# A fused two-block network on one Trainium2 core: the second score product on 128 rows, the shared buffer of the gating unit, and norm weights queued behind linear attention

## The chip, the core and the metric

One core of a Trainium2 chip runs the whole program in one launch. The metric is the device time of that launch in microseconds, the median over several runs. The core's engines are TensorE (PE in the profile, PEld for its weight loads), VectorE (DVE), ScalarE (ACT), GpSimd (POOL) and SyncE (SP), which here issues the DMAs. Each engine works through its own queue in order; the order is fixed when the program is built.

## What is computed

Two blocks follow each other on 256 tokens of width 1024.

- **First block**, two layers, on 256 latent tokens (x) and 256 context tokens (ctx). Each layer projects the modulated input and has three branches: softmax attention (8 query heads, 2 key/value heads of width 64), gated linear attention in both directions ("gla", 4 heads), and a spatial gating unit ("sgu"). The branches are multiplied with gates and summed ("merge"), projected, added to the residual and layer-normalised. In layer 0 latent and context rows are all kept (512 rows); layer 1 keeps the 256 latent rows only.
- **Second block**: forgetting attention, a linear recurrence, and a mixture of 32 experts whose weights (three matrices of 1 MB each) are all read from memory.

What the change touches, in the reference's words:

```python
def attend(q, k, v):
    s = jnp.einsum('btgrd,blgd->bgrtl', q, k, preferred_element_type=jnp.float32) * (ATTN_HEAD_DIM ** -0.5)
    p = jax.nn.softmax(s, axis=-1)
    return jnp.einsum('bgrtl,blgd->btgrd', p.astype(v.dtype), v)

y_sgu = sgu(s_u, s_v, ...) * jax.nn.silu(s_g)     # sgu: pu * (w_s @ layer_norm(pv) + b_s)
x_new = layer_norm(DEEPNORM_ALPHA * x + gate[:, None, :] * out, p['post_g'], p['post_b'])
```

## The kernel before

A large product keeps float32 accuracy by splitting each operand into a high part in the type fp32r and a low part (what is left), and adding three products: high x high, high x low, low x high. The weights are split on the core: ACT writes the high part (`whi`, L97), DVE or POOL subtracts (`wlo`, L98).

**Scores.** `attn_kv` (L531) makes the transposed keys. `kh` has the high part of both key heads; head h lies on 64 of the 128 rows, and POOL copies it to the other 64 (L547). `kl`, the low part, lies on its own 64 rows alone. `attn_core` (L626) takes 128 queries at a time (`tt`: four times in layer 0, twice in layer 1) and puts their high part on one half of the rows of `qs` and the low part on the other. Then there are four rounds (`r`) for each tt. A round makes the scores of two heads (g = 0, 1): one product with `kh` on 128 rows, which is high x high plus low x high at once (L644), and one with `kl` on 64 rows (L646). Softmax follows (DVE L651, L652, ACT L654, DVE L655, L656), four transposes per head (`trp`, PE L659), their copy (`pt`, ACT L661), and eight products with the values (`aops`, PE L666; each shows as two instructions). There are two buffers each for scores, softmax rows, transposes and copies. In layer 0, tt 0 and 1 look at 512 keys and tt 2 and 3 at 256; in layer 1 both look at 512. In all there are 24 rounds and 48 pairs of score products, 32 pairs with 512 columns and 16 with 256.

**Linear attention.** `gla_pair` takes two heads at a time and goes through eight levels (`LEVELS` and the diagonal): POOL (L827, L828, L830), ACT and DVE make the operands, PE the products `attps` (L841), DVE merges them (`accd`, L852). Then come the outputs `gops` (L863, L867) and per head a norm: ACT `osq` (L873), DVE `oms` (L875), POOL `ors` (a power, L222), DVE `on` (L879), POOL `on` (times the gate, L880), and PE transposes (`tro`, L883).

**Gating unit.** `sgu_core` makes `mxps` on PE (L950) for each tt, and both of the two `gm` banks of PSUM are taken by the products of two tt. DVE takes them into `mx` (L954, four instructions per tt), POOL multiplies (L957), ACT and DVE split the result into `ysg` (L958, L959).

**Merge.** `merge` runs twelve steps in the order of the string "s0 s1 s2 g0 g1 g2 a0 s3 g3 a1 a2 a3". A step has 48 gate products `mgps`, in two `gm` banks, and 24 branch products `brps`, on lines L247 to L249; s reads `ysg`, g reads `ygl`, a reads the attention's result.

**Norm weights.** While layer 1's merge begins, `first_block` (L1176, L1177) multiplies the residual x2 with the weights of layer 0's norm and adds its offset: four POOL instructions on 128x1024.

**What sets the order.** The program is written as a sequence, but the framework reorders it when it builds: each engine's queue is filled by a list schedule over the dependencies and the buffers. A tile of a rotating pool (`tmp` has three buffers per tag) is handed out in the program's order. `tc.issue_after(x)` puts what is issued in its block behind instruction x.

**Experts.** Their weights stream in from when the buffers of the earlier stages are given back, and `gu` (L1781) and `dnps` (L1836) use them; the last part of the program is paced by that stream.

Of the kernel before, what the change touches and what calls it, by code (L numbers as in the profile page):

```python
# [10 lines left out]
F32 = mybir.dt.float32  # L11
# [64 lines left out]
class Builder:  # L76
# [444 lines left out]
    def attn_tiles(self):  # L521
        L = self.L
        a1 = self.slot.tile([128, 2, 4, self.nx], F32, tag=self.half, bufs=self.nhalf, name="a1")
        L["a1"] = a1
        L["qT"], L["agT"] = a1[:, 0], a1[:, 1]

        L["kh"] = self.akv.tile([128, 2, 512], F32R, tag="kh", name="kh")
        L["kl"] = self.akv.tile([128, 512], F32R, tag="kl", name="kl")
        L["v"] = self.akv.tile([128, 4, 128], F32, tag="v", name="v")

    def attn_kv(self, t0, t1):  # L531
        nc, a, L = self.nc, self.a, self.L
        kh, kl, v = L["kh"], L["kl"], L["v"]
        tts = range(t0 // 128, t1 // 128)
        g = self.gemm_tok(self.chunk(a["w_in"][self.li], C_AK), tts)
        for tt in tts:
            kt = self.att.tile([128, 512], F32, tag="att2k", name="ktok")[:, :128]
            nc.scalar.activation(v[:, tt], g[tt][:, 128:256], AF.Copy)
            self.norm_rope(g[tt][:, 0:128], 2, 1, tt, kt.rearrange("p (h e) -> p h e", e=64))
            ps = self.ptr.tile([128, 128], F32, tag="tr", name="trk")  # L540
            nc.tensor.transpose(ps, kt, self.ident)
            ts = slice(tt * 128, tt * 128 + 128)
            for h in range(2):
                pr, other = slice(64 * h, 64 * h + 64), slice(64 - 64 * h, 128 - 64 * h)
                nc.scalar.activation(kh[pr, h, ts], ps[pr], AF.Copy)
                nc.vector.tensor_tensor(kl[pr, ts], ps[pr], kh[pr, h, ts].bitcast(F32), op=OP.subtract)
                nc.gpsimd.tensor_copy(kh[other, h, ts], kh[pr, h, ts])  # L547

    def attn_q(self):
        nc, a, L = self.nc, self.a, self.L  # L550
# [73 lines left out]
    def attn_core(self):  # L624
        nc, L = self.nc, self.L
        nq = self.nx // 128  # L626
        qT, kh, kl, v = L["qT"], L["kh"], L["kl"], L["v"]
        halves = [slice(64 * g, 64 * g + 64) for g in range(2)]
        y = L["y_a"] = self.slot.tile([128, 2, 4, self.nx], F32R, tag="slot", name="yat")
        for tt in range(nq):  # L630
            keys = (0, 512) if tt < 2 else (256, 512)
            nk = keys[1] - keys[0]
            nkc = nk // 128
            ops = self.pou.tile([128, 4, 128], F32, tag="ou", name="aops")

            qs = self.att.tile([128, 4, 2, 128], F32R, tag="qs", name="qs")
            for g in range(2):
                src, hi = qT[halves[g], :, tt * 128:tt * 128 + 128], qs[halves[g], :, g]
                nc.scalar.activation(hi, src, AF.Copy)  # L639
                nc.vector.tensor_tensor(qs[halves[1 - g], :, g], src, hi.bitcast(F32), op=OP.subtract)  # L640
            for r in range(4):
                sc = [self.psc.tile([128, 512], F32, tag="sc", name="asc")[:, :nk] for g in range(2)]
                for g in range(2):
                    nc.tensor.matmul(sc[g], qs[:, r, g], kh[:, g, keys[0]:keys[1]], start=True, stop=False)  # L644
                for g in range(2):
                    nc.tensor.matmul(sc[g], qs[halves[g], r, g], kl[halves[g], keys[0]:keys[1]], start=False, stop=True)  # L646
                pts = []
                for g in range(2):
                    s = sc[g]
                    st = self.sm.tile([128, 4], F32, tag="ast", name="ast")  # L650
                    nc.vector.tensor_reduce(st[:, 0:1], s, axis=AX.X, op=OP.max)  # L651
                    nc.vector.tensor_scalar(st[:, 1:2], st[:, 0:1], -0.125, None, op0=OP.mult)  # L652
                    p = self.att.tile([128, 512], F32, tag="att2k", name="p")[:, :nk]
                    nc.scalar.activation(p, s, AF.Exp, scale=0.125, bias=st[:, 1:2], accum_out=st[:, 2:3])  # L654
                    nc.vector.reciprocal(st[:, 3:4], st[:, 2:3])  # L655
                    nc.vector.tensor_scalar(p, p, st[:, 3:4], None, op0=OP.mult)  # L656
                    tp = self.ptr.tile([128, 4, 128], F32, tag="tr", name="trp")
                    for k in range(nkc):
                        nc.tensor.transpose(tp[:, k], p[:, k * 128:k * 128 + 128], self.ident)  # L659
                    pt = self.att.tile([128, 4, 128], F32, tag="pt", bufs=2, name="pt")  # L660
                    nc.scalar.activation(pt[:, :nkc], tp[:, :nkc], AF.Copy)  # L661
                    pts.append(pt)

                for k in range(nkc):
                    for g in range(2):
                        nc.tensor.matmul(ops[halves[g], r], v[:, keys[0] // 128 + k, 64 * g:64 * g + 64], pts[g][:, k],  # L666
                                         start=(k == 0), stop=(k == nkc - 1), skip_group_check=True)
            t = self.tmp.tile([128, 4, 128], F32, tag="tmp", name="yt")
            tc = slice(tt * 128, tt * 128 + 128)
            nc.vector.scalar_tensor_tensor(t, ops, 0.5, L["agT"][:, :, tc], op0=OP.mult, op1=OP.mult)  # L670
            nc.scalar.activation(y[:, 0, :, tc], t, AF.Copy)
            nc.vector.tensor_tensor(y[:, 1, :, tc], t, y[:, 0, :, tc].bitcast(F32), op=OP.subtract)
# [84 lines left out]
    def gla_pair(self, j):  # L757
# [111 lines left out]
        for h in range(2):  # L869
            hd = 2 * j + h  # L870
            ops = both[h]
            sq = self.tmp.tile([128, 4, 128], F32, tag="tmp", name="osq")[:, :nch]
            nc.scalar.activation(sq, ops, AF.Square, scale=128.0 ** -0.5)  # L873
            ms = self.sm.tile([128, 4], F32, tag="oms", name="oms")[:, :nch]
            nc.vector.tensor_reduce(ms, sq, axis=AX.X, op=OP.add)  # L875
            rs = self.sm.tile([128, 4], F32, tag="ors", name="ors")[:, :nch]
            self.rsqrt(rs, ms)
            on = self.tmp.tile([128, 4, 128], F32, tag="tmp", name="on")[:, :nch]
            nc.vector.tensor_tensor(on, ops, rs[:, :, None].to_broadcast([128, nch, 128]), op=OP.mult)  # L879
            nc.gpsimd.tensor_tensor(on, on, L["gg"][:, :nch, hd * 128:hd * 128 + 128], op=OP.mult)  # L880
            tp = self.ptr.tile([128, 4, 128], F32, tag="tr", name="tro")[:, :nch]
            for c in range(nch):
                nc.tensor.transpose(tp[:, c], on[:, c], self.ident)  # L883
            t = tp.rearrange("p c t -> p (c t)")
            yh, yl = L["y_g"][:, 0, hd], L["y_g"][:, 1, hd]
            nc.scalar.activation(yh, t, AF.Copy)
            nc.vector.tensor_tensor(yl, t, yh.bitcast(F32), op=OP.subtract)
# [56 lines left out]
    def sgu_core(self):  # L944
        nc, L = self.nc, self.L
        y = L["y_s"]
        for tt in range(self.nx // 128):
            ps = self.pgm.tile([128, 4, 128], F32, tag="gm", name="mxps")
            for g in range(4):
                nc.tensor.matmul(ps[:, g], L["vn"][:, tt, g * 128:g * 128 + 128], L["wsT"][:, g], start=True, stop=True,  # L950
                                 skip_group_check=True)
            t = self.att.tile([128, 4, 128], F32, tag="mx", bufs=1, name="mx")
            for g in range(4):
                nc.vector.scalar_tensor_tensor(t[:, g], ps[:, g], L["vT"][:, 28 + g:29 + g], L["sgr"][:, g],  # L954
                                               op0=OP.mult, op1=OP.add)
            tc = slice(tt * 128, tt * 128 + 128)
            nc.gpsimd.tensor_tensor(t, t, L["su"][:, :, tc], op=OP.mult)  # L957
            nc.scalar.activation(y[:, 0, :, tc], t, AF.Copy)  # L958
            nc.vector.tensor_tensor(y[:, 1, :, tc], t, y[:, 0, :, tc].bitcast(F32), op=OP.subtract)  # L959
# [108 lines left out]
    def first_block(self):  # L1068
        nc, tc, a = self.nc, self.tc, self.a
        with ExitStack() as st:  # L1070
# [92 lines left out]
            with ExitStack() as layer:  # L1163
# [6 lines left out]
                with ExitStack() as inner:  # L1170
# [1 line left out]
                    h2p = self.pool("h2T", side="right", stack=self.right, reuse_waits="tile")  # L1172
                    self.h2T = [h2p.tile([128, 8, 256], F32R, name=n) for n in ("h2Th", "h2Tl")]
                    pv = self.post_norm(0)
                    for t in range(2):
                        nc.gpsimd.tensor_tensor(x2[:, t], x2[:, t], pv[:, 0], op=OP.mult)  # L1176
                        nc.gpsimd.tensor_tensor(x2[:, t], x2[:, t], pv[:, 1], op=OP.add)  # L1177
                    pv = self.post_norm(1)
                    side = self.pool("lru", side="right", stack=self.right, reuse_waits="tile")
                    self.merge(iter(()))  # L1180
# [834 lines left out]
```

## Time and profile before

| what | value |
|---|---|
| three runs | 1340.64, 1340.48, 1337.61 us; median 1340.48 us |
| profiled execution | 1342.97 us, its span 1341.1 us |
| PE busy | 1253.8 us (93% of the span), 8099 instructions |
| DVE, ACT, POOL busy | 716.0, 578.4, 350.6 us |
| mean granted PE clock | 0.976 of full speed |
| DMA | 243.81 MB, mean 182 GB/s |

The spans and starts that follow are microseconds from the first instruction of the profiled execution. That execution took 2.49 us more than the median of the runs and 1.87 us more than its own span. A matmul's duration in the trace includes the drain, so successive ones overlap: what a matmul costs in a stream is the distance from its start to the next start. "Busy" of PE therefore hides short stalls.

### The profile page before, as it was taken

The numbers are of one execution on the slowest core, as the hardware profiler recorded it, in microseconds if no ns is written. First come the engines' busy times: TensorE is split into PE (matmuls) and PEld (weight loads), VectorE is DVE, ScalarE is ACT, GpSimd is POOL, SyncE is SP. The second block draws the span as 40 slices with busy tenths as digits, with TensorE's granted clock in tenths as the row PEclk, the third lists the DMA queues.
The fourth block names the chain that finished last, engine by engine and source line by source line (L and its number), as shares of the span: only waits on it lengthen the run. The fifth ranks groups of instructions, "written<-read, shape, count | busy, mean of one in ns | idle before, by whom it ended". The sixth has DMA issues, their size and how long they took to land. (4 is left out here: it accounts for less than half of the span.)

```text
span 1341.1 us, 21494 instructions
## 1 busy us (share of the span) xinstructions
PE 1253.8 (93%) x8099; PEld 934.1 (70%) x8099; DVE 716.0 (53%) x1412; ACT 578.4 (43%) x1099; POOL 350.6 (26%) x373
## 2 busy tenths in 40 slices
PE   5999999999999999999999989999799989999975
PEld 3679778777777666789887878799698685333221
DVE  2546585675553223368778777655787555111102
ACT  2463453535433222346776554544466434222201
POOL 2327743630000101143367455001054020000000
PEclk8999999999999999999999999999899989999988
DMA  9523232211114577545555435246469556999994
GB/s 309 187 64 100 78 90 69 64 47 54 58 48 120 182 240 229 175 157 157 160 165 156 136 96 188 79 118 179 145 243 331 167 200 256 410 409 408 409 409 180
DMA packets 169873, 243.81 MB, mean 182 GB/s; under 512 B 15285, under 2 KB 130205, under 8 KB 169761
## 3 DMA queue, kind: packets, MB, share of 16 engines
q1 hardware_dynamic: 169760, 242.35, 53.7%
q8 instruction: 66, 1.08, 0.3%
q14 instruction: 47, 0.38, 0.1%
HBM read 241.27 MB, written 1.05 MB: 181 GB/s over the span
## 5 line engine op out<-in xcount | busy, mean ns | idle before, releaser
L98 DVE TENSOR_TENSOR wlo<-raw,whi 128x1024 fp32r<-128x1024 f32 (+1 forms) x202 | 251.6, 1250 | 153.0 <-ACT whi L97 151.4
L97 ACT ACTIVATE whi<-raw 128x1024 fp32r<-128x1024 f32 (+1 forms) x216 | 212.6, 993 | 197.5 <-PE mgps L248 35.1
L247 PE MATMUL mgps<-hTh,whi 128*128 128x512 f32 (+1 forms) x384 | 133.6, 349 | 4.9 <-DVE msum L991 2.6
L249 PE MATMUL mgps<-hTh,wlo 128*128 128x512 f32 (+1 forms) x384 | 132.0, 347 | 0.1
L248 PE MATMUL mgps<-hTl,whi 128*128 128x512 f32 (+1 forms) x384 | 131.7, 343 | 0.0
L994 POOL TENSOR_TENSOR msum<-msum,tanh 128x512 f32<-128x512 f32 (+1 forms) x32 | 35.2, 1104 | 343.6 <-DVE tanh L993 325.9
L1781 PE MATMUL gups<-gu,xw 128*64 128x512 f32 (+1 forms) x512 | 100.2, 618 | 6.4 <-DMA gu<-w_up 6.4
L247 PEld LDWEIGHTS mgps<-hTh,whi 128*128 128x128 f32 x384 | 73.4, 192 | 19.6 <-issue 6.2
L249 PEld LDWEIGHTS mgps<-hTh,wlo 128*128 128x128 f32 x384 | 73.3, 191 | 11.7 <-issue 3.6
L248 PEld LDWEIGHTS mgps<-hTl,whi 128*128 128x128 f32 x384 | 73.6, 192 | 9.0 <-issue 1.9
L1781 PEld LDWEIGHTS gups<-gu,xw 128*64 128x64 f32 (+1 forms) x512 | 25.3, 124 | 60.7 <-issue 58.9
L298 PE MATMUL gmt<-whi,hTh 128*128 128x512 f32 x160 | 61.2, 398 | 2.6 <-ACT qs L639 1.3
L299 PE MATMUL gmt<-wlo,hTh 128*128 128x512 f32 x160 | 62.8, 393 | 0.3 <-DVE wlo L98 0.2
L222 POOL TENSOR_TENSOR frs<-rsq,mhalf 128x1 f32<-128x1 f32 x2 | 1.1, 547 | 235.3 <-DVE frs L1955 235.3
L300 PE MATMUL gmt<-whi,hTl 128*128 128x512 f32 x160 | 62.5, 391 | 0.0
L1813 DVE SCALAR_TENSOR_TENSOR eth<-eth,gups 128x256 f32<-128x256 f32 x12 | 5.1, 421 | 102.3 <-ACT eth L1812 102.3
L1836 PE MATMUL dnps<-dn,hm 128*64 128x512 f32 (+1 forms) x256 | 51.4, 610 | 5.1 <-DMA dn<-w_down 5.1
L651 DVE TENSOR_REDUCE ast<-asc 128x1 f32<-128x512 f32 (+1 forms) x48 | 28.6, 600 | 42.2 <-PE asc L646 42.1
L661 ACT ACTIVATE pt<-trp 128x512 f32<-128x512 f32 (+1 forms) x48 | 24.9, 526 | 56.2 <-PE trp L659 50.7
L283 PE MATMUL gmt<-wlo,hTh 128*128 128x256 f32 x160 | 45.7, 286 | 1.8 <-DVE wlo L98 1.8
L98 DVE TENSOR_TENSOR ol<-dnps,oh 128x512 fp32r<-128x512 f32 x24 | 16.6, 690 | 57.2 <-ACT oh L97 57.2
L282 PE MATMUL gmt<-whi,hTh 128*128 128x256 f32 x160 | 45.4, 284 | 0.6 <-ACT g L742 0.6
(571 smaller groups left out, 3282.4 us busy)
## 6 DMA issues: line engine op xcount, KB each, us to landing
raw<-w_in SPq DMA_DIRECT2D x132, 512.0 KB
gu<-w_gate SPq DMA_DIRECT2D x64, 512.0 KB
gu<-w_up SPq DMA_DIRECT2D x64, 512.0 KB
dn<-w_down SPq DMA_DIRECT2D x28, 1024.0 KB
adar<-w_ada SPq DMA_DIRECT2D x32, 512.0 KB
raw<-w_out SPq DMA_DIRECT2D x32, 512.0 KB
adaw<-w_ada SPq DMA_DIRECT2D x16, 512.0 KB
raw<-w_in SPq DMA_DIRECT2D x32, 256.0 KB
```

The lines of the kernel that those rows point to most:

```text
L97: nc.scalar.activation(hi, x, AF.Copy)
L98: return (eng or nc.vector).tensor_tensor(lo, x, hi.bitcast(F32), op=OP.subtract).ins
L247: nc.tensor.matmul(ps, wh, xh, start=(u == 0 and k == 0), stop=False)
L248: nc.tensor.matmul(ps, wh, xl, start=False, stop=False)
L249: nc.tensor.matmul(ps, wl, xh, start=False, stop=(u == len(acts) - 1 and k == 3))
L282: nc.tensor.matmul(out[tt], xh, hi[:, j, :n], start=first, stop=False, skip_group_check=True)
L283: nc.tensor.matmul(out[tt], xh, lo[:, j, :n], start=False, stop=False, skip_group_check=True)
L298: nc.tensor.matmul(out[tt], xh, hi[:, j], start=(i == 0 and j == 0), stop=False)
L299: nc.tensor.matmul(out[tt], xh, lo[:, j], start=False, stop=False)
L300: nc.tensor.matmul(out[tt], xl, hi[:, j], start=False, stop=(i == 3 and j == 1))
L1781: mm = nc.tensor.matmul(u["ps"][pr], u["x"][:, k, pr], u["gu"][ei][k // 4][:, :, k % 4], start=(k == 0), stop=(k == 7), skip_group_check=T ...
L1836: mm = nc.tensor.matmul(ps[pr], hm[:, f, pr], dns[ei][:, f, 512 * hf:512 * hf + 512], start=(f == 0), stop=(f == 1), skip_group_check=True ...
```

## The change

It has three parts. (1) `kl` gets a second half like `kh`: 16 more POOL copies (two for each of four tt in each layer), and the second score product is on all 128 rows. Since `qs` has the high part on one half and the low part on the other, the product now also adds low x low. The four score products of a round are written head by head. (2) `kl` takes 2 KB more per partition. The gating unit's `mx` loses its own buffer (pool `att`, tag `mx`) and takes a buffer of the rotating pool `tmp`, which is also used by attention's `yt`. (3) The four POOL instructions of the norm weights stand behind the last `on` of layer 1's linear attention.

```diff
-        L["kl"] = self.akv.tile([128, 512], F32R, tag="kl", name="kl")
+        L["kl"] = self.akv.tile([128, 2, 512], F32R, tag="kl", name="kl")
...
-                nc.vector.tensor_tensor(kl[pr, ts], ps[pr], kh[pr, h, ts].bitcast(F32), op=OP.subtract)
+                nc.vector.tensor_tensor(kl[pr, h, ts], ps[pr], kh[pr, h, ts].bitcast(F32), op=OP.subtract)
                 nc.gpsimd.tensor_copy(kh[other, h, ts], kh[pr, h, ts])
+                nc.gpsimd.tensor_copy(kl[other, h, ts], kl[pr, h, ts])
...
                 for g in range(2):
-                    nc.tensor.matmul(sc[g], qs[:, r, g], kh[:, g, keys[0]:keys[1]], start=True, stop=False)
-                for g in range(2):
-                    nc.tensor.matmul(sc[g], qs[halves[g], r, g], kl[halves[g], keys[0]:keys[1]], start=False, stop=True)
+                    for kx in (kh, kl):
+                        nc.tensor.matmul(sc[g], qs[:, r, g], kx[:, g, keys[0]:keys[1]], start=(kx is kh), stop=(kx is kl))
...
-            nc.gpsimd.tensor_tensor(on, on, L["gg"][:, :nch, hd * 128:hd * 128 + 128], op=OP.mult)
+            self.last_on = nc.gpsimd.tensor_tensor(on, on, L["gg"][:, :nch, hd * 128:hd * 128 + 128],
+                                                   op=OP.mult).ins
...
-            t = self.att.tile([128, 4, 128], F32, tag="mx", bufs=1, name="mx")
+            t = self.tmp.tile([128, 4, 128], F32, tag="tmp", name="mx")
...
-                    for t in range(2):
-                        nc.gpsimd.tensor_tensor(x2[:, t], x2[:, t], pv[:, 0], op=OP.mult)
-                        nc.gpsimd.tensor_tensor(x2[:, t], x2[:, t], pv[:, 1], op=OP.add)
+                    with tc.issue_after(self.last_on):
+                        for t in range(2):
+                            nc.gpsimd.tensor_tensor(x2[:, t], x2[:, t], pv[:, 0], op=OP.mult)
+                            nc.gpsimd.tensor_tensor(x2[:, t], x2[:, t], pv[:, 1], op=OP.add)
```

The built order of the engines shows more than the diff. Three places follow; in the changed program the scores are both on L646, and the lines behind them are one to three higher.

PE's queue in layer 0's attention before (`asc` scores, `trp` transposes of the softmax, `aops` products with the values, `brps` and `mgps` the merge's products):

```order
L247 MATMUL brps<-ysg,whi 128x512
L248 MATMUL brps<-ysg,whi 128x512
L249 MATMUL brps<-ysg,wlo 128x512
L666 MATMUL aops<-pt,v 64x128 x7
L644 MATMUL asc<-kh,qs 128x512
L646 MATMUL asc<-kl,qs 128x512
L659 MATMUL trp<-ident,p 128x128 x4
L644 MATMUL asc<-kh,qs 128x512
L646 MATMUL asc<-kl,qs 128x512
L247 MATMUL mgps<-hTh,whi 128x512
L248 MATMUL mgps<-hTl,whi 128x512
L249 MATMUL mgps<-hTh,wlo 128x512
```

and in the changed program, where the rows from the first softmax transposes on read:

```order
L659 MATMUL trp<-ident,p 128x128 x8
L666 MATMUL aops<-pt,v 64x128
L646 MATMUL asc<-kh,qs 128x512
L646 MATMUL asc<-kl,qs 128x512
L659 MATMUL trp<-ident,p 128x128 x4
L666 MATMUL aops<-pt,v 64x128 x7
L646 MATMUL asc<-kh,qs 128x512
L646 MATMUL asc<-kl,qs 128x512
L659 MATMUL trp<-ident,p 128x128 x4
L646 MATMUL asc<-kh,qs 128x512
L646 MATMUL asc<-kl,qs 128x512
L666 MATMUL aops<-pt,v 64x128 x8
```

The merge's products no longer stand between the attention's steps, neither here nor in layer 1; all of them stand behind the last `aops` of the layer.

PE's queue in layer 0 where the first merge products come in, before:

```order
L644 MATMUL asc<-kh,qs 128x512
L646 MATMUL asc<-kl,qs 128x512
L950 MATMUL mxps<-wsT,s_1446 128x128 x4
L247 MATMUL mgps<-hTh,whi 128x512
L248 MATMUL mgps<-hTl,whi 128x512
L249 MATMUL mgps<-hTh,wlo 128x512
```

and in the changed program:

```order
L666 MATMUL aops<-pt,v 64x128 x4
L659 MATMUL trp<-ident,p 128x128 x4
L666 MATMUL aops<-pt,v 64x128 x4
L951 MATMUL mxps<-wsT,s_1454 128x128 x8
L247 MATMUL mgps<-hTh,whi 128x512
L248 MATMUL mgps<-hTl,whi 128x512
L249 MATMUL mgps<-hTh,wlo 128x512
```

Before, the gating unit's last `mxps` and the first `mgps` stood right behind the first scores. Now two of the four `mxps` still stand ahead of attention, the other two and all `mgps` behind its end; DVE's queue has all the `mx` rows behind the last `yt`.

POOL's queue at the end of layer 1's linear attention (`ors`, `on` its norm, `x_3443` the residual, `post` the norm weights), before:

```order
L830 TENSOR_TENSOR klv<-klv,g_5626 128x256 x2
L222 TENSOR_TENSOR ors<-rsq,mhalf 128x2
L1176 TENSOR_TENSOR x_3443<-x_3443,post 128x1024 x2
L880 TENSOR_TENSOR on<-on,g_5627 128x256
L222 TENSOR_TENSOR ors<-rsq,mhalf 128x2
L1177 TENSOR_TENSOR x_3443<-x_3443,post 128x1024 x2
L880 TENSOR_TENSOR on<-on,g_5627 128x256
L994 TENSOR_TENSOR msum<-msum,tanh 128x256 x6
```

and in the changed program:

```order
L830 TENSOR_TENSOR klv<-klv,g_5634 128x256
L222 TENSOR_TENSOR ors<-rsq,mhalf 128x2
L880 TENSOR_TENSOR on<-on,g_5635 128x256
L222 TENSOR_TENSOR ors<-rsq,mhalf 128x2
L880 TENSOR_TENSOR on<-on,g_5635 128x256
L1179 TENSOR_TENSOR x_3451<-x_3451,post 128x1024 x2
L1180 TENSOR_TENSOR x_3451<-x_3451,post 128x1024 x2
L1215 MEMSET r2T 128x4x3
L958 TENSOR_TENSOR mx<-mx,s_6674 128x512 x2
L995 TENSOR_TENSOR msum<-msum,tanh 128x256 x16
```

The four norm instructions moved from between the two heads' `ors` and `on` to behind them, and the two `mx` products of the gating unit, which stood a few rows above this piece, to behind the norm instructions.

## Rows read from the trace of the kernel before

**Rows 1.** Windows, all engines: us, busy us (count) of PE, PEld, DVE, ACT, POOL; clock, DMA

```profile
275.50:422.50 147.00, 145.15 (x772) 105.77 (x770) 80.57 (x188) 63.97 (x138) 14.32 (x12) 0.99 0.18 54
774.90:829.90 55.00, 49.08 (x469) 43.38 (x470) 43.08 (x81) 25.35 (x55) 33.06 (x29) 0.97 0.44 130
829.90:884.50 54.60, 54.60 (x417) 43.94 (x416) 31.93 (x69) 28.52 (x57) 4.57 (x7) 1.00 0.33 101
1150.00:1310.00 160.00, 146.50 (x750) 49.02 (x746) 27.01 (x74) 32.93 (x95) 0.00 (x0) 0.97 1.03 409
```

**Rows 2.** Windows, of line L247's instructions alone, same columns

```profile
275.50:422.50 147.00, 49.25 (x121) 23.02 (x121) 0.99 0.18 54
774.90:829.90 55.00, 26.30 (x88) 17.09 (x88) 0.97 0.44 130
829.90:884.50 54.60, 19.39 (x66) 12.36 (x66) 1.00 0.33 101
```

**Rows 3.** Timeline of PE in layer 0's attention: start, duration, line, operation, tiles, shapes

```profile
302.75 0.39 PE L249 MATMUL brps<-ysg,wlo 128*128 128x512 f32 x1
302.98 0.60 PE L659 MATMUL trp<-ident,p 128*128 128x128 f32 x4
303.51 0.43 PE L666 MATMUL aops<-pt,v 128*64 128x128 f32 x2
303.87 0.50 PE L644 MATMUL asc<-kh,qs 128*128 128x512 f32 x1
304.30 0.49 PE L646 MATMUL asc<-kl,qs 64*128 64x512 f32 x1
304.72 0.66 PE L659 MATMUL trp<-ident,p 128*128 128x128 f32 x4
...
308.06 1.09 PE L666 MATMUL aops<-pt,v 128*64 128x128 f32 x14
```

**Rows 4.** Instruction groups of DVE, 275 to 430: line, tiles, shapes, count, busy us, mean ns

```profile
L651 DVE TENSOR_REDUCE ast<-asc 128x1 f32<-128x512 f32 x16 | 11.0, 690 | 18.7 <-PE asc L646 18.7
...
L954 DVE SCALAR_TENSOR_TENSOR mx<-mxps,vT,sgr 128x128 f32<-128x128 f32 x12 | 3.4, 343 | 0.1
```

**Rows 5.** Instruction groups of ACT, 275 to 430, same columns

```profile
L654 ACT ACTIVATE p<-asc,ast 128x512 f32<-128x512 f32 x16 | 11.0, 686 | 1.9 <-DVE ast L652 1.9
L661 ACT ACTIVATE pt<-trp 128x512 f32<-128x512 f32 x16 | 9.4, 597 | 22.9 <-PE trp L659 22.5 <-ACT whi L97 0.3
```

**Rows 6.** Timeline of PE in layer 0 between linear attention and the merge

```profile
281.02 0.71 PE L867 MATMUL gops<-g,acc 128*128 128x128 f32 x4
...
286.20 0.50 PE L247 MATMUL mgps<-hTh,whi 128*128 128x512 f32 x1 [1.85 <-DVE mx L954]
```

**Rows 7.** Windows of two stretches behind that wait, columns as in rows 1

```profile
287.50:290.50 3.00, 3.00 (x8) 2.30 (x7) 2.29 (x6) 0.63 (x1) 2.73 (x3) 0.50 0.00 0
290.50:293.50 3.00, 3.00 (x15) 2.47 (x14) 1.46 (x3) 0.63 (x1) 2.54 (x2) 0.95 0.00 0
```

**Rows 8.** Timeline of POOL in layer 1's second pair of heads

```profile
775.80 1.06 POOL L827 TENSOR_TENSOR klv<-g 128x128 f32<-128x128 f32 x1 [0.97 <-PE trkh L783]
...
791.21 2.44 POOL L830 TENSOR_TENSOR klv<-klv,g 128x256 f32<-128x256 f32 x2
811.55 1.77 POOL L222 TENSOR_TENSOR ors<-rsq,mhalf 128x2 f32<-128x2 f32 x1 [17.90 <-DVE rsq L221]
814.08 4.77 POOL L1176 TENSOR_TENSOR x<-x,post 128x1024 f32<-128x1024 f32 x2 [0.76 <-DMA post<-post_ln_g]
...
827.85 1.71 POOL L880 TENSOR_TENSOR on<-on,g 128x256 f32<-128x256 f32 x1
```

**Rows 9.** Timeline of DVE ahead of and beside the norm weights

```profile
811.54 1.23 DVE L98 TENSOR_TENSOR wlo<-raw,whi 128x1024 fp32r<-128x1024 f32 x1
...
817.07 4.54 DVE L98 TENSOR_TENSOR wlo<-raw,whi 128x1024 fp32r<-128x1024 f32 x2 [0.56 <-ACT whi L97]
```

## The prediction

> **What bounds the kernel now.** I read the windows by stage first. In layer 0's attention PE is busy for 145.15 of 147.00 us, in layer 1's second pair of linear attention for 49.08 of 55.00, in layer 1's attention all the time, while DVE, ACT and POOL each have slack [rows 1]. In the last window the DMA engines are full (share 1.03, 409 GB/s): there the expert weights set the pace, and they start when earlier stages give their buffers back. So I take it that a microsecond lost or won in the first two layers is lost or won at the end, one for one.
>
> Next, what keeps PE busy. The merge's products stand between the softmax steps: 121, 88 and 66 of line L247 in the three windows, each beside one of L248 and one of L249, so 363, 264 and 198 products [rows 2]. They follow one another at 0.23 us with 512 columns (302.75 to 302.98, [rows 3]); I take 0.12 for layer 1's 256 columns, half of that. They are filler: while a head's scores go through DVE and ACT (reduction 0.690, exponential 0.686, copy of the transposes 0.597, [rows 4, 5]) PE works on them. Without them the stages' own lengths are
>
> - layer 0: 147.0 - 363 x 0.23 = 63.5 us,
> - layer 1: 55.0 - 264 x 0.12 = 23.3 and 54.6 - 198 x 0.12 = 30.8, together 54.1 us.
>
> **Part 1, the scores.** A pair of `kh` and `kl` takes 303.87 to 304.72 = 0.85 us, 0.43 and 0.42 [rows 3], where a full product in a stream takes 0.23. I put the excess down to the change between 128 and 64 rows on each side of `kl`; on 128 rows there is none. The trace has no `kl` on 128 rows: at best a pair takes 2 x 0.23 = 0.46, at worst 0.85 as now. I take 0.55, near the row of the stream, with some excess left because transposes stand on either side. For 48 pairs that is up to 48 x 0.30 = 14 us of PE; it is contained in the round lengths below.
>
> The trace has no case of two `kl` side by side. The Trainium skill, TensorEngine Tiling (Array Packing), Key Properties, says that tiles on different rows of the array work in parallel and that switching the mode drains the engine. By the first half two 64-row products would share one slot, and the change would cost 24 x 0.23 = 5.5 us rather than win 14; [rows 3] speak against it here, since each `kl` stands alone, and for the second half.
>
> The 16 added copies are POOL passes; the nearest row is 1.06 us for 128x128 [rows 8], so 0 to 17 us. They precede attention, POOL works 14.32 of 147.00 us in layer 0's window [rows 1], and keys are ready well ahead of the scores: 0, covered by the other PE work there.
>
> **Part 2, `mx` in the rotating buffers, is the larger one.** By the built order two of the four `mxps` hold both `gm` banks until their `mx` has run, and DVE has every `mx` behind the last `yt`. So all the filler of a layer now stands behind the last `aops`: attention runs bare, and the merge pays its full length afterwards. The products removed above return one for one, so only the stages' own lengths count.
>
> A bare round with 512 keys has on PE 2 x 0.55 scores, 2 x 0.53 transposes (302.98 to 303.51), 0.36 (303.51 to 303.87) and 1.09 for the two and the fourteen `aops` [rows 3]: 3.61 us. DVE and ACT have twice 0.69 and twice (0.69 + 0.60) = 2.6 plus short steps [rows 4, 5], in parallel for two heads. PE is the longest if the order overlaps the heads well: **3.6 us**, between 2.9 (short pairs, overlapped drains) and 4.4 (one head's chain waits for the other's). With 256 keys half would be 1.8; hand-offs don't halve, so I take 2.45, up to 3.0.
>
> Layer 0, its own length now:
>
> - 275.5 to the last `gops`, 281.0 + 0.5 = 281.5 [rows 6]: 6.0; then the norms of two heads, `ors` 1.77 and `on` 1.71 each (prices of layer 1, [rows 8]) = 7.0, and 1.5 for the first softmax: 14.5
> - 8 x 3.6 + 8 x 2.45 + 2 x 1.4 at the start and turn of the key length = 51.2
> - the last chain's end 1.0, and the gap before the first `mgps` gets a bank: twelve `mx` at 0.343 [rows 4] = 4.1, with `yt` and hand-offs ahead of them 5.2
> - the clock behind that gap. Before, a wait of 1.85 us for `mx` at 286.20 [rows 6] was followed by 3 us at a granted clock of 0.50 (1.2 GHz of 2.4), 8 products against 15 in the next 3 us [rows 7]: 1.5 lost.
>
> That makes 14.5 + 51.2 + 1.0 + 5.2 + 1.5 = 73.4 against 63.5: **+9.9**.
>
> Layer 1: the second pair runs bare. POOL's levels take 775.80 to 791.21 + 2.44 = 793.65, 17.9 and the two norms 2 x (1.77 + 1.71) = 7.0 [rows 8], 25.0 with little overlap; then 8 x 3.6 + 0.7 = 29.5, end 1.0, gap before the merge 2.0 (four `mx` at 0.343 and hand-offs). That is 57.5.
>
> **Part 3, the norm weights.** They go from between the norms to behind them. Before, they began at 814.08 after a wait of 0.76 for a transfer, and put 4.77 and about as much again into the chain that ends with `on` at 827.85 + 1.71 [rows 8]. But in that time PE worked on filler [rows 1], so taking it out wins nothing that the 25.0 does not hold already. They now lie beside the softmax on DVE. There two `wlo` took 4.54, 2.27 each, against 1.23 for one just ahead of them [rows 9]. The norm weights' 2 x 4.77 = 9.5 us would cover three rounds; DVE's 3 us per round at up to 1.85 times gives 0 to +7.5; I take 1.5, since a round has some slack on DVE. POOL's `mx` and `msum` queue behind them, which only the merge awaits. Layer 1: 57.5 + 1.5 - 54.1 = **+4.9**.
>
> **Sum:** 0 + 9.9 + 4.9 = +14.8 on the profiled execution's 1342.97, so 1357.8. That execution is 2.49 over the median of the runs; on the median's basis **1355.3 us**. A measurement of this kernel can tell about 0.3%, 4 us, from no change.
>
> **Rivals.**
>
> - *Slower by far: bare rounds lose the clock.* PE waits in every round, if a head's chain does not overlap the other's: 4.4 and 3.0 us, 16 x 0.8 + 8 x 0.55 = 17.2 more. For it: ACT's `pt` waited 22.5 us for `trp` in all [rows 5], and the 0.50 behind the 1.85 us [rows 7]. Against: PE has 3.6 us of its own work per round, so gaps are short. [...] 1357 + 17 to **1372**, chance 0.14.
> - *The pair of scores stays at 0.85.* Then the excess comes from the work on either side of it and not from the 64 rows, and a round has 0.6 (512 keys) or 0.3 more: 16 x 0.6 + 8 x 0.3 = 12, **1367**. Against: a full product between others takes 0.23 [rows 3]. Chance 0.06. The skill's rule above would have it so where it lets 64-row products share a slot.
> - *No change:* rounds at 3.2 and 2.0, 16 x 0.4 + 8 x 0.45 = 10 less, and gaps of 2 less per layer: 14.8 - 14 = +1, **1341**. Bounded by the score pair: it needs 0.46 or drains hidden. Chance 0.18.
> - *Faster: the score pairs pay in full and the bare stages don't wait.* Rounds at 2.9 and 1.8 (16 x 0.7 + 8 x 0.65 = 16.4 less) and 10 less in the norms and gaps, because the second pair's POOL levels no longer share PE's queue with filler: -12, **1329**. It decides at rounds under 3.0 and 2.0. For it: DVE and ACT alone need only 2.6. Chance 0.15.
> - *The change doesn't do what it says:* the norm wait wins nothing, as taken above; that is part of the forecast.
>
> **How the numbers follow.** The forecast has 0.47, with a range of its own from 1347 to 1364 (the bounds of the pair, the gap and the norm weights). The 8 in 10 range reaches down to no change and up to the slow rival: 1336 to 1372; left out are the faster case and the tail above. Faster by over 0.3% (below 1336.5): 0.15, within 0.18, slower 0.67.
>
> **What would show it.** `asc` of `kl` should start within 0.3 us of that of `kh`, and the pair end at 0.46 to 0.60. The windows of the attention should hold no L247 at all, PE less than 95% busy, a clock under 0.99. The distance from one round's last `aops` to the next's gives the round, 3.6 or not. Behind the last `aops` of layer 0 PE should wait about 5 us for DVE's `mx`. In layer 1 the last `tro` should follow `on` without the norm weights, and DVE's passes beside these should be longer. The forecast falls if the stages' own lengths come out below 63.5 and 54.1, or if the time changes elsewhere than in these stages, such as in the expert stream, which would break the one-for-one rule.

## The result: 1.6% slower, and the profile after

The changed kernel takes 1359.45 us in the median of four runs (1356.28 to 1362.55), the kernel before 1339.05 in four. The ratio is 1.0158, 95% interval 1.0140 to 1.0176: 20 us slower, where +14.8 was forecast and 1336 to 1372 was the range.

The profiled execution of the changed kernel took 1356.28 us, span 1354.5, which is 13.4 more than the span before. The two profiled executions lie on different sides of their medians (before 3.9 us over 1339.05, after 3.2 under 1359.45), which is why the medians lie 20 apart and the profiles 13. By stages, from the starts in the two traces (a last `brps` by its end):

| stage | before | after | difference | forecast |
|---|---|---|---|---|
| start to layer 0's first `asc` | 275.5 | 271.9 | -3.6 | 0 |
| layer 0, first `asc` to last `brps` | 299.5 | 311.5 | +12.0 | +9.9 |
| between the layers | 186.6 | 187.3 | +0.7 | 0 |
| layer 1, first `gops` to last `brps` | 175.1 | 179.6 | +4.5 | +4.9 |
| from there to the end | 404.4 | 404.2 | -0.2 | 0 |

The -3.6 is in a part that the change hardly touches. The same part came out 1.8 shorter in the run of part 3 alone (below), whose queues up to layer 1 are those of the kernel before, and PE's waits for the transfer of `w_ada` near the start fell from 10.3 to 7.6 us. So most of it is variation between executions. The two layers together came to +16.5 where +14.8 was forecast.

The windows of the changed kernel, all engines (us, then busy us and count of PE, PEld, DVE, ACT, POOL; granted clock, DMA share, GB/s), answer to [rows 1]:

```profile
271.90:290.30 18.40, 10.54 (x66) 7.66 (x65) 9.36 (x23) 6.25 (x13) 4.90 (x5) 0.83 0.07 23
290.30:323.00 32.70, 31.22 (x233) 21.92 (x232) 25.05 (x74) 23.54 (x55) 0.00 (x0) 0.94 0.01 2
323.00:341.70 18.70, 16.17 (x108) 9.99 (x105) 13.29 (x52) 11.45 (x41) 0.00 (x0) 1.00 0.00 1
341.70:348.40 6.70, 2.22 (x18) 1.95 (x17) 6.54 (x18) 1.89 (x3) 2.50 (x2) 1.00 0.63 195
348.40:583.40 235.00, 232.93 (x1200) 175.91 (x1201) 72.53 (x96) 63.66 (x84) 27.32 (x18) 0.99 0.50 156
770.70:799.60 28.90, 21.26 (x276) 18.89 (x275) 19.88 (x49) 14.38 (x39) 18.08 (x28) 0.88 0.32 92
799.60:812.90 13.30, 9.05 (x46) 6.28 (x44) 7.72 (x23) 4.88 (x12) 5.53 (x6) 0.76 0.24 81
812.90:843.30 30.40, 29.39 (x225) 20.78 (x224) 22.03 (x55) 18.88 (x46) 7.04 (x4) 0.94 0.13 36
...
1165.00:1325.00 160.00, 145.99 (x742) 48.54 (x738) 27.02 (x74) 32.51 (x94) 0.00 (x0) 0.96 1.03 408
```

What was one stage of 147 us with PE busy all but 1.85 of them is now a start (18.4 us, PE busy 10.5), the rounds (51.4, PE 47.4), a gap (6.7, PE 2.2) and then the merge. The expert stream of the last row is what it was: 1.03 and 408 GB/s.

Line L247 alone in the same kernel, in layer 0 from the first `asc` to the first `mgps`, and in layer 1 from the first `gops` to the last `aops`:

```profile
271.90:348.40 76.50, 0.01 (x1) 0.01 (x1) 0.93 0.07 24
770.70:843.30 72.60, 6.97 (x24) 4.60 (x24) 0.88 0.22 67
```

121 merge products of L247 before [rows 2], none now; the one in the first row is that of 348.39 on its edge. The 24 in layer 1 are products of the gating unit's own projection (`sgps`) and not of the merge, whose first `mgps` starts at 845.1.

PE's timeline in layer 0 (start, duration, line, operation, tiles, shapes; in brackets how long it had waited and for what) shows the start, the pair of scores and the gap:

```profile
283.50 0.74 PE L884 MATMUL tro<-ident,on 128*128 128x128 f32 x4 [4.80 <-POOL on L880]
286.74 1.11 PE L884 MATMUL tro<-ident,on 128*128 128x128 f32 x4 [2.50 <-POOL on L880]
...
294.55 0.50 PE L646 MATMUL asc<-kh,qs 128*128 128x512 f32 x1
294.88 0.40 PE L646 MATMUL asc<-kl,qs 128*128 128x512 f32 x1
295.12 0.60 PE L659 MATMUL trp<-ident,p 128*128 128x128 f32 x4
...
343.53 2.19 PE L951 MATMUL mxps<-wsT,s 128*128 128x128 f32 x16 [1.82 <-DVE mx L955]
348.39 0.50 PE L247 MATMUL mgps<-hTh,whi 128*128 128x512 f32 x1 [2.66 <-DVE mx L955]
```

The pair takes 295.12 - 294.55 = 0.57 us, against 0.85 [rows 3]. What a change of rows costs could be read before the change, in linear attention, where groups of products on 64 and on 128 rows alternate (the kernel before, timeline of PE):

```profile
280.60 0.49 PE L863 MATMUL gops<-S,qin 64*128 64x128 f32 x4
281.02 0.71 PE L867 MATMUL gops<-g,acc 128*128 128x128 f32 x4
```

Inside a group on 128 rows the starts are 0.11 us apart; the last start before a change of rows and the first one after it are each followed by a distance 0.1 longer. So a change costs about 0.2 us, and `kl` between two products on 128 rows has two of them: 0.4, which is 0.85 less 2 x 0.23.

In front, PE waits 7.3 us for the two `on`, which the merge's products covered before; behind, it waits 4.5 us in two pieces for `mx`. DVE's timeline in that gap:

```profile
341.75 0.69 DVE L670 SCALAR_TENSOR_TENSOR yt<-aops,a 128x512 f32<-128x512 f32 x1 [1.72 <-PE aops L666]
342.36 2.15 DVE L955 SCALAR_TENSOR_TENSOR mx<-mxps,vT,sgr 128x128 f32<-128x128 f32 x8
344.57 0.48 DVE L1318 MEMSET bd_w_a<- 128x512 f32 x1
345.11 0.48 DVE L1318 MEMSET bd_w_x<- 128x512 f32 x1
345.51 1.19 DVE L672 TENSOR_TENSOR yat<-yt,yat 128x512 fp32r<-128x512 f32 x1
346.62 0.68 DVE L960 TENSOR_TENSOR ysg<-mx,ysg 128x512 fp32r<-128x512 f32 x1
347.22 1.11 DVE L955 SCALAR_TENSOR_TENSOR mx<-mxps,vT,sgr 128x128 f32<-128x128 f32 x4
```

The order is the one read from the build: the last `yt`, eight `mx`, and four more before a bank is free. But two memsets of the next stage, `yat` and `ysg` stand between the eighth and the ninth, 2.7 us that PE waits for as well. Behind the gap the clock is low as before behind a wait [rows 7] (windows, PE alone):

```profile
349.00:352.00 3.00, 3.00 (x8) 0.50 0.04 9
352.00:355.00 3.00, 3.00 (x14) 0.97 0.30 88
```

POOL in layer 1 (timeline), from the first level of the second pair of heads on, where the norm weights are now behind the last `on`:

```profile
784.05 1.22 POOL L827 TENSOR_TENSOR klv<-g 128x128 f32<-128x128 f32 x1 [1.25 <-PE trkh L783]
...
795.88 0.72 POOL L830 TENSOR_TENSOR klv<-klv,g 128x256 f32<-128x256 f32 x1 [0.64 <-ACT klv L829]
806.13 0.69 POOL L222 TENSOR_TENSOR ors<-rsq,mhalf 128x2 f32<-128x2 f32 x1 [9.52 <-DVE rsq L221]
807.36 0.72 POOL L880 TENSOR_TENSOR on<-on,g 128x256 f32<-128x256 f32 x1 [0.54 <-DVE on L879]
808.19 0.70 POOL L222 TENSOR_TENSOR ors<-rsq,mhalf 128x2 f32<-128x2 f32 x1
809.49 0.72 POOL L880 TENSOR_TENSOR on<-on,g 128x256 f32<-128x256 f32 x1 [0.60 <-DVE on L879]
810.16 4.67 POOL L1179 TENSOR_TENSOR x<-x,post 128x1024 f32<-128x1024 f32 x2
814.80 5.04 POOL L1180 TENSOR_TENSOR x<-x,post 128x1024 f32<-128x1024 f32 x2
```

and DVE beside them (timeline; the last row is the first of the kind behind them):

```profile
813.41 1.71 DVE L656 TENSOR_SCALAR p<-p,ast 128x512 f32<-128x512 f32 x1
...
815.70 1.91 DVE L656 TENSOR_SCALAR p<-p,ast 128x512 f32<-128x512 f32 x1
...
818.79 1.33 DVE L656 TENSOR_SCALAR p<-p,ast 128x512 f32<-128x512 f32 x1
...
820.83 0.49 DVE L656 TENSOR_SCALAR p<-p,ast 128x512 f32<-128x512 f32 x1
```

`ors` and `on` take 0.7 each where they took 1.7 [rows 8]; three passes over the softmax rows on DVE take up to four times their 0.49. PE in the first round there:

```profile
814.70 1.91 PE L666 MATMUL aops<-pt,v 128*64 128x128 f32 x14
```

### The profile page after: what moved, and what is told of

Same layout as the page of the kernel before. It is cut to its first block, busy times and chain, and to the rows that moved or that the text cites. A ratio compares the mean times of both kernels' runs of the same rounds, so it can differ in the third digit from the quotient of the medians.

```text
span 1354.5 us, 21548 instructions
## 1 busy us (share of the span) xinstructions
PE 1246.5 (92%) x8099; PEld 936.6 (69%) x8099; DVE 715.8 (53%) x1412; ACT 578.8 (43%) x1099; POOL 344.4 (25%) x389
## 3 DMA queue, kind: packets, MB, share of 16 engines
q8 instruction: 66, 1.08, 0.3%
## 5 line engine op out<-in xcount | busy, mean ns | idle before, releaser
L98 DVE TENSOR_TENSOR wlo<-raw,whi 128x1024 fp32r<-128x1024 f32 (+1 forms) x202 | 247.9, 1232 | 202.8 <-ACT whi L97 201.3
L247 PE MATMUL mgps<-hTh,whi 128*128 128x512 f32 (+1 forms) x384 | 131.0, 342 | 4.6 <-DVE mx L955 4.5
L247 PEld LDWEIGHTS mgps<-hTh,whi 128*128 128x128 f32 x384 | 73.3, 191 | 15.9 <-DVE mx L955 4.9
L284 PE MATMUL gmt<-whi,hTl 128*128 128x256 f32 x160 | 45.5, 284 | 0.0
L1830 ACT ACTIVATE hm<-hmps 128x256 f32<-128x256 f32 x12 | 4.6, 383 | 86.5 <-PE hmps L1825 86.5
```

Of the source, the lines that this page charges most:

```text
L98: return (eng or nc.vector).tensor_tensor(lo, x, hi.bitcast(F32), op=OP.subtract).ins
L247: nc.tensor.matmul(ps, wh, xh, start=(u == 0 and k == 0), stop=False)
```

## The experiments

The theory to be tested, called M: part 2 alone makes the loss, since it takes the filler out of attention; part 1 is a gain of 32 x 0.26 + 16 x 0.25 = 12 us; part 3 is nothing. The rivals put the loss on part 1 (S) or on part 3 (N). In the table, layer 0 is from the first `asc` to the last `brps` and layer 1 from the first `gops` to the last `brps`, in us of the profiled execution.

| kernel | parts | `mx` in | ratio to before, 95% | layer 0 | layer 1 |
|---|---|---|---|---|---|
| before | - | its own | 1 | 299.5 | 175.1 |
| after | 1, 2, 3 | `tmp` | 1.0158 (1.0140 to 1.0176) | 311.5 | 179.6 |
| e1 | 3 | its own | 1.0031 (1.0014 to 1.0048) | 303.4 | 173.2 |
| e2 | 2 | `tmp` | 1.0319 (1.0281 to 1.0358) | 325.8 | 195.4 |
| e3 | 1 | `vn` | 0.9948 (0.9927 to 0.9970) | 296.1 | 168.3 |
| e4 | 1, 3 | `vn` | 0.9922 (0.9892 to 0.9953) | 295.8 | 164.8 |
| e5 | 1, 2 | `tmp` | 1.0218 (1.0169 to 1.0266) | 311.0 | 190.1 |
| e6 | 2, 3 | `tmp` | 1.0357 (1.0290 to 1.0424) | 333.1 | 183.5 |
| e7 | none | `vn` | 1.0065 (1.0035 to 1.0095) | 308.7 | 173.4 |
| e8 | 1, 2, 3 | `tmp`, ahead of `yt` | 0.9993 (0.9966 to 1.0020) | 294.6 | 176.8 |
| e9 | 1 in part, 2, 3 | `tmp` | 1.0210 (1.0166 to 1.0255) | 320.8 | 183.5 |
| e10 | 1 in part, 2, 3 | `tmp` | 1.0150 (1.0111 to 1.0189) | 314.8 | 180.3 |

**e1, part 3 alone.** The kernel before with the norm weights in `tc.issue_after(self.last_on)`, as in the change's diff, and nothing else.

> The kernel before with part 3 alone: the four norm-weight instructions behind the last `on`. Theory M (the whole loss comes from `mx` in the rotating buffers, since that takes the filler out of attention): 300 and 175 merge products stay inside the two attentions, so no change, ratio 0.997 to 1.003, although the chain of layer 1's second pair is freed of 9.5 us of POOL work. Rival N (the late norm weights slow DVE's passes or hold up POOL's `mx` and `msum`, and that is a share of the loss): +4 us or more, ratio 1.003 to 1.01.

Measured: +0.31% (0.14 to 0.48), 4 us, on the edge between M and N. In the trace layer 1 is 1.9 shorter, not longer, and the 3.9 us of layer 0 lie where the queues are those of the kernel before; so the late norm weights are not seen to cost anything where N says they do, and where the 4 us of the median come from stays open. Freeing the chain of 9.5 us of POOL work won at most 1.9 us behind filler.

**e2, part 2 alone.**

```diff
-            t = self.att.tile([128, 4, 128], F32, tag="mx", bufs=1, name="mx")
+            t = self.tmp.tile([128, 4, 128], F32, tag="tmp", name="mx")
```

> The kernel before with part 2 alone: `mx` in the rotating buffers, `kl` on 64 rows. No merge product is left inside either attention. Theory M: the loss of the whole change plus what the scores give back, 32 pairs x 0.26 + 16 x 0.25 = 12 us (0.83 to 0.57 and 0.61 to 0.36 in the two profiles), so +32 us, 1371 us, ratio 1.02 to 1.027. Rival S (the 128-row scores, their copies and the low x low product cause the loss): no change, ratio 0.997 to 1.003. Rival L (bare rounds are limited by DVE and ACT, and the shorter scores win nothing there): +20 us, ratio 1.013 to 1.017.

Measured: +3.19% (2.81 to 3.58), 43 us and not 32; S and L fall. Part 2 makes more than the whole loss, and parts 1 and 3 together give back some 22. The trace has two reasons for the 11 us too many. In layer 1 the first `asc` to the first `aops` takes 25.0 us against 13.3 in the changed kernel, mostly because here the norm weights still stand between the norms (e5, the changed kernel with them there, takes 23.0). And in layer 0 the rounds with 256 keys run mostly at the low clock (1.2 GHz of 2.4). The two are worth 11.7 and 11.5 us in this execution; M had 4 of the second, so they more than cover the 11. The windows of the 512-key and the 256-key rounds, PE alone, of e2:

```profile
290.60:324.70 34.10, 33.79 (x218) 0.91 0.01 1
324.70:356.80 32.10, 30.86 (x120) 0.59 0.00 1
```

and of the changed kernel:

```profile
290.30:321.10 30.80, 29.32 (x218) 0.94 0.01 1
321.10:341.70 20.60, 18.07 (x120) 1.00 0.00 1
```

32.1 against 20.6 us for the same 120 instructions: a granted clock of 0.59 against 1.00, although PE is busy for 96% of the stretch. e9 and e10 take this up.

**e3, part 1 alone.** The kernel before with the change's `kl` and a place for `mx` that costs no buffer: the rows of `vn` that the product `mxps` of the same tt has just read.

```diff
-            t = self.att.tile([128, 4, 128], F32, tag="mx", bufs=1, name="mx")
+            t = L["vn"][:, tt].rearrange("p (g d) -> p g d", g=4)
```

> Part 1 alone: `kl` on 128 rows, and `mx` written over the rows of `vn` that its own product has just read, so that it needs no buffer at all and none of attention's. 304 and 192 merge products stay inside the two attentions. Theory M: PE is the bound in these stages again and the shorter pairs are won in full, -12 us, 1327 us, ratio 0.989 to 0.993. Rival S: no gain or a loss, ratio 0.998 to 1.015.

Measured: -0.52% (0.30 to 0.73), 7 us; S falls, but the size is short of the band. The control e7 has the reason: `mx` in `vn` costs 0.65% by itself. Against that, part 1 is worth 0.9948 / 1.0065 = 0.988, 16 us, give or take 5, which holds the forecast 12; the two layers of the traces differ by 12.6 and 5.1. With filler on both sides a pair takes 0.55 us (median of the 16 in layer 1).

**e4, parts 1 and 3 with `mx` in `vn`**, that is the changed kernel with that one line of e3 in place of the tmp buffer.

> The whole change but with `mx` over the rows of `vn` instead of in the rotating buffers: parts 1 and 3. Theory M: as part 1 alone, -12 us, ratio 0.989 to 0.993, and within 0.3% of it. Rival N: 4 us or more slower than part 1 alone. If the loss is in part 2, this differs from the changed kernel by 30 us.

Measured: -0.78% (0.47 to 1.08), 10 us under the kernel before and about 31 under the changed kernel, from which it differs by one line. That is the loss, with its place. It is the fastest kernel of the study. Part 3 is within 0.3% of nothing here too.

**e5, parts 1 and 2**, the changed kernel without `issue_after`.

> Parts 1 and 2 without part 3. Theory X (part 3 wins nothing behind filler, but in the bare second pair of layer 1 the norm weights stand in the chain between the norms: first `asc` to first `aops` took 25.0 us in part 2 alone and 13.3 in the changed kernel): the changed kernel + 11.7 us, 1371 us, ratio 1.022 to 1.028. Rival P (the parts simply add, and part 3 costs the 0.3% it cost alone): 0.3% under the changed kernel, ratio 1.011 to 1.014.

Measured: 1.0218 (1.0169 to 1.0266), at the lower edge of X and above P. Layer 1 is 10.5 longer than in the changed kernel (190.1 against 179.6), and layer 0 is the same. POOL's timeline shows the place:

```profile
805.78 0.70 POOL L222 TENSOR_TENSOR ors<-rsq,mhalf 128x2 f32<-128x2 f32 x1 [9.54 <-DVE rsq L221]
808.21 2.34 POOL L1176 TENSOR_TENSOR x<-x,post 128x1024 f32<-128x1024 f32 x1 [1.73 <-DMA post<-post_ln_g]
...
814.15 4.64 POOL L1177 TENSOR_TENSOR x<-x,post 128x1024 f32<-128x1024 f32 x2
818.75 0.73 POOL L880 TENSOR_TENSOR on<-on,g 128x256 f32<-128x256 f32 x1
```

The second `on` ends at 819.5, 13.7 us after the first `ors` began; in the changed kernel 4.1 (806.13 to 810.2). So part 3 is worth 10 us of this chain once PE has no filler to put there (0.6%, 8 us, by the ratios), and nothing that shows while it has. The fourteen `aops` of the first round took 1.91 us in the changed kernel, and here, with PE already at the full clock:

```profile
823.52 1.09 PE L666 MATMUL aops<-pt,v 128*64 128x128 f32 x14
```

**e6, parts 2 and 3**, the changed kernel with the scores of the kernel before.

> Parts 2 and 3 with `kl` on 64 rows. Theory X: against part 2 alone layer 1 wins 11.7 us, and against the changed kernel the bare rounds lose what part 1 gave, 66.2 against 51.4 us of attention in layer 0 and 32.9 against 30.3 in layer 1, 17 us: 1377 us, ratio 1.026 to 1.031; and the 256-key rounds of layer 0 run at a granted clock near 0.55 again. Theory M as it stood (12 us for the scores, bare or not): ratio 1.023 to 1.026. Rival P: 1.034 or more.

Measured: 1.0357 (1.0290 to 1.0424); its interval holds the end of X's band and P's too, so the total decides nothing. M falls. In the trace layer 1 wins 11.9 against e2, as X says, but layer 0 is 7.3 longer than in e2 (333.1 against 325.8), which takes most of it back: its first two distances from round to round are 7.2 us each (4.6 and 4.1 in e2), all at the low clock although PE is busy throughout (windows, PE alone):

```profile
291.80:306.00 14.20, 14.20 (x56) 0.50 0.01 1
```

The rounds with 256 keys run at 0.62, where X has 0.55. The runs behind the ratio spread widely, from 1374.7 to 1395.3.

**e7, `mx` in `vn` alone**, the line of e3 in the kernel before.

> The kernel before with `mx` written over the rows of `vn`, nothing else: the control for the two runs in which part 1 had its `mx` there. Theory M: ratio 0.997 to 1.003, so that the 0.5% of part 1 is its own. Rival V (a place for `mx` per `tt` in the stead of one buffer lets the merge begin earlier): 0.992 to 0.997, and part 1 is worth nothing by itself.

Measured: +0.65% (0.35 to 0.95); M and V fall alike. What PE waited for in layer 0 (waits: engine, line, what for, us in total, times, longest), e7, where the kernel before has no wait for `whi`:

```profile
PE brps L247 <- ACT whi L97: 3.4, 2, 2.5
PE mgps L247 <- ACT whi L97: 2.9, 1, 2.9
```

The merge begins at 279.2 instead of 286.2, and later runs into weights that have not come: 6.3 us. e4 has the same two waits (3.2 and 3.2). e3 and e4 leave part of their gain in layer 0 there; why the weights come later there was not tried.

**e8, the changed kernel with another order of writing.** All three parts and the tmp buffers stay; the gating unit is written ahead of attention, so that its `mx` are handed their buffers before the `yt`.

```diff
-            self.attn_core()
             self.sgu_proj()
             self.sgu_core()
+            self.attn_core()
```

> The changed kernel, all three parts and `mx` in the rotating buffers, but with the gating unit's two steps written ahead of attention in the program, so that its `mx` get their buffers before the `yt`: 310 and 198 merge products stand inside the two attentions. Theory M (it is the order in which the rotating buffers are handed out and nothing else of part 2): as parts 1 and 3 with `mx` over `vn`, ratio 0.988 to 0.997. Rival R (sharing three buffers costs by itself, since `yt` and `mx` wait for one another): 1.003 or more.

Measured: 0.9993 (0.9966 to 1.0020). R falls: 508 filler products are back inside the two attentions (between the first and the last `aops`), and 1.0158 - 0.9993 = 1.65%, 22 us, are won against the changed kernel, all that it had lost. So it is the order in which the rotating buffers are handed out, and not their being shared; that the unit's other steps move ahead in the program as well is not separated from it. It stays above M's band: the filler begins at 290.3 and 796.0, against 280.5 and 774.2 in e4, so that the norms of layer 0 (a wait of 4.8 us for `on`) and most of layer 1's second pair still run bare.

**e9 and e10, the clock of the bare rounds.** The changed kernel with the second score product on 64 rows again in layer 0's 512-key rounds (e9) or in its 256-key rounds (e10). Of the edit, the lines that choose the rows:

```diff
+                    pr = halves[g] if self.nx == 512 and tt < 2 else slice(0, 128)
+                    nc.tensor.matmul(sc[g], qs[pr, r, g], kl[pr, g, keys[0]:keys[1]], start=False, stop=True)
```

(e9's; e10 has `tt >= 2`.)

> The changed kernel with the second score product on 64 rows again in layer 0's rounds with 512 keys, on 128 in its rounds with 256 keys and in layer 1. Theory C (bare rounds fall to the low clock by what they themselves run, and with 128 rows they hold it): the seven 512-key distances take 29 us (26.4 in the changed kernel), the seven 256-key ones 18.5 at a granted clock near 1.00, and the time is that of the changed kernel + 3 us. Rival H (the low clock of the 256-key rounds comes from what ran ahead of them): 28 us for the 256-key ones at a clock near 0.55, + 13 us.

> The changed kernel with 64 rows again in layer 0's rounds with 256 keys only. Theory C: the seven 512-key distances stay at 26.4 us, the seven 256-key ones take 28 us (18.5 in the changed kernel) at a granted clock near 0.55, and the time is that of the changed kernel + 10 us. Rival H: 22 us at most at a clock above 0.9, 16 pairs x 0.25 = 4 us more than in the changed kernel.

Measured: e9 1.0210 (1.0166 to 1.0255), e10 1.0150 (1.0111 to 1.0189). Of e9's time 3.9 us are in layer 1, whose code is that of the changed kernel, so the totals tell less than the windows. The windows of the 512-key and the 256-key rounds of e9, PE alone:

```profile
292.50:332.40 39.90, 39.24 (x218) 0.75 0.00 1
332.40:353.30 20.90, 18.20 (x121) 1.00 0.01 1
```

and of e10:

```profile
291.60:322.80 31.20, 30.23 (x218) 0.93 0.00 1
322.80:346.00 23.20, 21.12 (x121) 1.00 0.00 1
```

Each theory is right in one run and wrong in the other: in e9 the 256-key rounds keep the full clock, as C says, and in e10 they keep it too, as H says. C's 29 us for e9's seven 512-key distances fall as well: they take 35.0, the first two at the low clock as in e6. The low clock came in the 256-key rounds only where these and the rounds ahead of them had 64 rows (e2, e6), and in the 512-key rounds it was longest in e6 and e9 (0.75 in both), though e2 has the same products there (0.91). Layer 1's bare rounds have 64-row products too in e2 and e6, and ran at 0.92 and 0.98, against 0.94 in the changed kernel. So in these runs long stretches of bare rounds at the low clock came only with 64-row products, but not with all of them, and neither their place nor what ran ahead settles it. Which further condition decides stays open.

## Why the prediction was right, and where its steps were off

- **What bounds it, and one for one.** Right. Without filler the stage's length is its own; the 363 products came back behind it: 235.0 us of merge against 152.5 before (from the last `aops`, 422.5, to 575.0), and 152.5 + 83.5 = 236.0. From the end of layer 1's merge both kernels take 404 us.
- **Part 1.** Right in size: pairs of 0.57, forecast 0.55, and 16 us behind filler (e3 over e7). The change of rows on each side of `kl` is what goes, and its price of 0.2 us in linear attention's products accounts for the excess; the Trainium skill's rule on that (TensorEngine Tiling (Array Packing), Key Properties, where switching the mode drains the engine) agrees with 0.85 to 0.57. The rule on a shared slot has a case that the prediction passed over: the `gops` products on 64 rows shown above lie by twos on different halves of the rows, the two start 6 or 7 ns apart, and the four with their change of rows take 0.42 us (280.60 to 281.02). An estimate from these numbers: `kh`, `kh`, `kl`, `kl` with the two `kl` side by side would take 3 x 0.23 + 2 x 0.2 = 1.1 us, where the four took 2 x 0.85 and now take 2 x 0.57, without a second half of `kl` and so without a buffer to find for it; it was not tried. The rival that the pair stays at 0.85 falls.
- **Part 2, the rounds.** 26.4 / 7 = 3.77 us for 512 keys in layer 0 (from the last `aops` of one round to that of the next), forecast 3.6; 18.5 / 7 = 2.64 for 256, forecast 2.45. That is 1.2 and 1.3 us over the seven distances; with the turn of the key length (2.2) shorter than counted, layer 0's rounds from the first `aops` on take 51.4 where 51.2 and 1.0 were forecast.
- **Part 2, start and gap.** The start was sized 14.5 and took 18.4: the two norms were priced at POOL's `ors` and `on` alone, without ACT's and DVE's steps between them, and from the end of the last `gops` (277.8) to the second `tro` (286.74) it took 9.0 us where 7.0 was sized; from there to the first `aops` it took 3.6 where 1.5 was. The gap was sized 5.2 and took 6.7: "with `yt` and hand-offs ahead of them" left out the passes that DVE's queue has between the eighth and ninth `mx`. The clock behind the gap cost what [rows 7] promised, 8 products in 3 us. Together they make 5.4 us too few; the rounds and the merge behind (235.0 where 236.0 and 1.5 were forecast) give 3.3 back, which leaves the 2.1 by which layer 0 came out over its forecast.
- **Layer 1's sum.** The total came out (+4.5, forecast +4.9), but by errors that cancel, which is luck. From POOL's first `klv` to the end of the last `on` it took 26.2 us, sized 25.0; in it the levels took 12.6 and not 17.9, the norms 4.1 and not 7.0, and between them POOL waited 9.5 us for the products and the steps of the norm on other engines. [rows 8] show that wait (17.90), and the sum has no term for it. Up to the first `mgps` (845.07) it is 61.0 us where 57.5 and 1.5 were sized; the merge behind, 105.2, is 2.0 shorter than its 51.8 before and the 462 x 0.12 that came back.
- **Part 3.** The term beside DVE is not contradicted. Passes of 0.49 went up to 1.91, more than the 1.85 times of [rows 9]. From the first `aops` to the last, layer 1 takes 30.05 us against 28.72 in e5, where the norm weights are done before: 1.3 more, where 1.5 was sized. All but 0.2 of it is in the first round, in which PE was also at the low clock for longer than in e5 (`aops` of 1.91 against 1.09), so how much of it DVE's passes make stays open. And "taking it out wins nothing that the 25.0 does not hold already" hid a dependence: it wins 10 us only because part 2 had bared that chain (e5), and nothing behind filler (e1, e4).
- **The rivals.** The slower one, bare rounds at the low clock (its 1372 is 1355 + 17, on the median's basis, and not 1357 + 17), did not come in the changed kernel (0.94 and 1.00), but it is real: with 64 rows the 256-key rounds take 32.1 us and not 20.6 (e2), though not for the waits that the rival names, since PE is busy there for 96%. No change and faster fall; they needed rounds of 3.2 and under 3.0.

## What to carry to other kernels

Before a buffer is put into a shared rotating pool, look at where in the program its new neighbours are handed theirs: here the products that filled PE's waits stood behind a bank that was held by a buffer handed out after attention, and one line cost 31 us. Memory that is free already (rows that the producing step has just read) or another order of writing keeps the gain. And price each part of a change in the state that the others leave: moving POOL work out of a chain was worth nothing behind filler and 10 us without it.

## What was not expected of the hardware

A stretch with PE busy for 96% of its time ran at a granted clock of 0.59 when the second score product had 64 rows, and at 1.00 with 128, where PE was busy for 88% (e2 and the changed kernel, 120 instructions, 32.1 and 20.6 us); in e6 14 us of PE without a pause ran at 0.50. DVE passes over 128x512 beside POOL's passes over 128x1024 took 1.3 to 1.9 us in the place of 0.49, and POOL's small `ors` and `on` took 0.7 where, beside other DVE work, they had taken 1.7.
